# Strassen's scheme moved from the down projections to the gate and up projections of both SwiGLU layers

## The chip, the cores and the metric

The kernel runs on one core of a Trainium2 chip. Times are microseconds (us) of that core for one launch; the hardware profiler also records one execution, whose span (first to last instruction) and own time are given below. TensorE is PE in the rows, its weight loads PEld, VectorE DVE, ScalarE ACT, GpSimd POOL, and SP is the engine whose queue issues the loads.

## The reference

One decoder layer on 512 tokens of width 1024, all in float32: a SwiGLU layer, a token mixer (a gated linear recurrence beside stick-breaking attention, not touched here), and a second SwiGLU layer. The inner width of a SwiGLU layer is 2816.

```python
def _swiglu(x, w_gate, w_up, w_down):
    return (jax.nn.silu(x @ w_gate) * (x @ w_up)) @ w_down

x = x + 0.5 * _swiglu(_rms_norm(x, ffn1_norm), ffn1_w_gate, ffn1_w_up, ffn1_w_down)
...   # the mixer
x = x + 0.5 * _swiglu(_rms_norm(x, ffn2_norm), ffn2_w_gate, ffn2_w_up, ffn2_w_down)
```

## The kernel before

Activations lie transposed: 8 tiles (k = 0 to 7) of 128 channels x 512 tokens. The inner width is cut into 22 blocks of 128, taken in chunks of 6, 6, 6 and 4 blocks (`CHUNKS`). SwiGLU layer "a" is the first, "b" the second; the letter is in the names of the tiles (`pga`, `l_gb`), and so is the number of the block or chunk in the source's names, which the profile leaves out.

Every float32 operand is split in two: a rounded high part (a cast on ACT) and the remainder (a subtraction on DVE), and every product is made of three matmuls, high x high, high x low, low x high (`mm3`, and the three-fold loop in `product`). `weights` loads a weight tile through the SP queue and `parts` splits it; the split tiles have four buffers each (`wh`, `wl`), so the split of a weight tile waits until PE has used the tile four places before it.

`products(f)` makes gate and up of one block plainly: 2 matrices x 8 k x 3 matmuls of 512 columns. `hidden` multiplies by the norm factor `rb`, applies silu as a sigmoid and a product, and multiplies gate by up. The norm factor comes late (`rsqrt`, `spread`), so the first blocks are multiplied before it is there.

The down projection of the first three chunks uses Strassen's scheme in Winograd's form (7 products instead of 8): the 2 x 2 blocks are the inner blocks f and f+1 of a pair, the output tiles k and k+4, and the two halves of 256 tokens. `operands` makes the activations' seven combinations of a pair and splits them (`bh`, `bl`); `down` adds the weights (`sums`, DVE), splits four groups of them, and runs 7 products of m = 3 pairs x 3 matmuls of 256 columns, each collected into `x` by DVE (`collect`, L350). The last chunk of 4 blocks goes down plainly (`down_plain`).

The order on each engine is made when the program is built: a scheduler takes the instructions in the order of the source and issues those that are ready first by its own model; on the chip each engine then runs its list in that order. `products` of the next chunk stands ahead of a chunk's down projection, so that PE has work while the activations are combined.

Of the kernel before, what the change touches and what calls it, by code (L numbers as in the profile page):

```python
# [28 lines left out]

ORDER = (0, 4, 1, 5, 2, 6, 3, 7)  # L30
# [19 lines left out]
def hybrid_layer_kernel(  # L50
# [160 lines left out]

    def ffn(name, xn, wg, wu, wd, first, done):
        def products(f, between=None):
            n = f"{name}{f}"
            gh, gl = weights(wg[f], f"g{n}")
            uh, ul = weights(wu[f], f"u{n}")
# [16 lines left out]
        with tc.tile_pool(name=f"ffn_{name}", bufs=2, reuse_waits="tile") as fp:  # L233

            def hidden(f, out_):

                n = f"{name}{f}"
                if f == len(ahead):
                    ahead.append(products(f))
                pg, pu = ahead[f]  # L240
                g = fp.tile([P, T], F32, tag="g", name=f"gg{n}")
                nc.vector.tensor_mul(g, pg, rb)
                sg = fp.tile([P, T], F32, tag="sg", name=f"sg{n}")
                nc.scalar.activation(sg, g, AF.Sigmoid)
                u = fp.tile([P, T], F32, tag="u", name=f"uu{n}")
                nc.vector.tensor_mul(u, pu, rb)  # L246
                nc.vector.tensor_mul(u, u, g)
                hidden.last = nc.vector.tensor_mul(out_, halves(u), halves(sg))

            def halves(ap):  # L250
                return ap.rearrange("p (c t) -> p c t", c=2)

            def operands(f, i):

                n = f"{name}{f}"

                b = fp.tile([P, 8, TH], F32, tag="b", name=f"b{n}")
                hidden(f, b[:, 0:2, :][:, ::-1, :])
                hidden(f + 1, b[:, 2:4, :])
                nc.vector.tensor_sub(  # L260
                    b[:, 4:8:2, :], b[:, 1:4:2, :], b[:, 0:1, :].to_broadcast([P, 2, TH])
                )
                for o, t, m in ((5, 4, 3), (7, 5, 2)):
                    nc.vector.scalar_tensor_tensor(
                        b[:, o, :], b[:, t, :], -1.0, b[:, m, :], op0=ALU.mult, op1=ALU.subtract
                    )
                h = fp.tile([P, 7, TH], F32R, tag=f"bh{i}", name=f"bh{n}", bufs=1)
                l = fp.tile([P, 7, TH], F32R, tag=f"bl{i}", name=f"bl{n}", bufs=1)
                for c in (slice(0, 3), slice(3, 7)):
                    r = b[:, c.start + 1 : c.stop + 1, :]  # L270
                    nc.scalar.copy(h[:, c, :], r)
                    nc.vector.tensor_sub(l[:, c, :], r, f32(h[:, c, :]))
                return h, l

            def plain(f, i):

                n = f"{name}{f}"
                b = fp.tile([P, 2, TH], F32, tag="h", name=f"hf{n}")
                hidden(f, b)
                if i % 2 == 0:  # L280
                    plain.tiles = [
                        fp.tile([P, 7, TH], F32R, tag=f"b{c}{i // 2}", name=f"h{c}{n}", bufs=1) for c in "hl"
                    ]
                h, l = (t[:, i % 2 * 2 : i % 2 * 2 + 2, :] for t in plain.tiles)
                nc.scalar.copy(h, b)
                nc.vector.tensor_sub(l, b, f32(h))
                return h.rearrange("p c t -> p (c t)"), l.rearrange("p c t -> p (c t)")

            def down_plain(k, col, nf, hs):

                n = f"{name}{col}_{k}"
# [17 lines left out]
                if done is not None:  # L309
                    done(k)  # L310
# [645 lines left out]
```

## Time and profile before

| | |
|---|---|
| time, median of 3 runs | 944.76 us (939.89 to 945.4) |
| profiled execution | 943.62 us, span 941.8 us |
| granted TensorE clock | 0.995 |
| busy: PE, PEld, DVE, ACT, POOL | 927.3, 785.5, 670.6, 374.1, 110.9 us |
| loaded from memory | 86.54 MB |
| layer a, mixer, layer b (by the chain's rows) | about 0 to 350, 350 to 585, 585 to 942 us |

Matmuls are pipelined: the duration of one (390 ns for 512 columns, 284 ns for 256) is longer than the distance from its start to the next one's start, so work on PE is counted here by distances of starts. The same holds in a small way for DVE, whose instructions start some 0.08 us before the one ahead has ended.

### The profile page before, as it was taken

What the parts mean: (1) busy time and instruction counts of PE and PEld (TensorE: products, weight loads), DVE (VectorE), ACT (ScalarE), POOL (GpSimd) and SP (SyncE); (2) the same over time, 40 slices, a digit from 0 to 9 for tenths busy, and PEclk for the clock granted to TensorE, in tenths of its full rate; (3) what the DMA queues carried; (4) which work ended last, traced back from release to release, by engine and by line L of the source; (5) the groups of instructions that cost most, each with busy time, mean ns of one, the idle gap of its engine ahead of it and who ended that gap; (6) DMA issues with size and microseconds to landing.
All of it is one profiled execution on the core that took longest, in us unless ns stands there. A gap on an engine that the chain in (4) does not pass through costs nothing.

```text
span 941.8 us, 12498 instructions
## 1 busy us (share of the span) xinstructions
PE 927.3 (98%) x4906; PEld 785.5 (83%) x4906; DVE 670.6 (71%) x1001; ACT 374.1 (40%) x528; POOL 110.9 (12%) x79
## 2 busy tenths in 40 slices
PE   8999999999999999999999999999999999999998
PEld 6888988898889888888776567888988899889987
DVE  7696867686768649855768868387766777677753
ACT  7233433333333326446556744343333334333430
POOL 4000000000000004644431140500000000000000
PEclk9999999999999999999998999999999999999999
DMA  7530342035202423322110122421253125212312
GB/s 246 179 112 1 130 162 94 19 114 178 90 23 68 142 82 112 112 89 90 34 56 24 46 80 93 164 90 45 68 179 104 53 68 179 90 68 68 111 46 90
DMA packets 27066, 89.44 MB, mean 95 GB/s; under 512 B 3072, under 2 KB 5376, under 8 KB 27008
## 3 DMA queue, kind: packets, MB, share of 16 engines
q1 hardware_dynamic: 27008, 88.65, 27.6%
q8 instruction: 39, 0.64, 0.3%
q14 instruction: 19, 0.16, 0.0%
HBM read 86.54 MB, written 2.10 MB: 94 GB/s over the span
## 4 chain that ended last, share of the span: by engine, by line
PE 90%; DVE 4%; issue 2%; DMA 1%; ACT 1%; POOL 1%; SPq 1%; DVEq 0%; ACTq 0%; POOLq 0%
PE pda L343 10%; PE pdb L343 9%; PE pga L137 5%; PE pga L138 5%; PE pga L139 5%; PE pub L137 4%; PE pub L138 4%; PE pub L139 4%; PE pgb L137 4%; PE pgb L139 4%; PE pgb L138 4%; PE pua L138 4%; PE pua L137 4%; PE pua L139 4%; PE po L137 1%
## 5 line engine op out<-in xcount | busy, mean ns | idle before, releaser
L343 PE MATMUL pdb<-bhb,h_db 128*128 128x256 f32 x252 | 71.2, 284 | 0.0
L343 PE MATMUL pda<-bha,h_da 128*128 128x256 f32 x252 | 71.2, 284 | 0.0
L343 PE MATMUL pdb<-blb,h_db 128*128 128x256 f32 x252 | 71.0, 283 | 0.0
L343 PE MATMUL pda<-bla,h_da 128*128 128x256 f32 x252 | 71.0, 283 | 0.0
L343 PE MATMUL pdb<-bhb,l_db 128*128 128x256 f32 x252 | 70.5, 284 | 0.2 <-DVE l_db L129 0.2
L343 PE MATMUL pda<-bha,l_da 128*128 128x256 f32 x252 | 70.4, 283 | 0.0
L137 PE MATMUL pub<-xh_b,h_ub 128*128 128x512 f32 x176 | 68.7, 390 | 0.5 <-DVE yo L704 0.5
L137 PE MATMUL pgb<-xh_b,h_gb 128*128 128x512 f32 x176 | 68.7, 390 | 0.0
L139 PE MATMUL pgb<-xh_b,l_gb 128*128 128x512 f32 x176 | 68.5, 389 | 0.0
L139 PE MATMUL pub<-xh_b,l_ub 128*128 128x512 f32 x176 | 68.5, 389 | 0.0
L138 PE MATMUL pgb<-xl_b,h_gb 128*128 128x512 f32 x176 | 68.5, 389 | 0.0
L138 PE MATMUL pub<-xl_b,h_ub 128*128 128x512 f32 x176 | 68.5, 389 | 0.0
L137 PE MATMUL pga<-xh_a,h_ga 128*128 128x512 f32 x160 | 62.4, 390 | 0.0
L137 PE MATMUL pua<-xh_a,h_ua 128*128 128x512 f32 x160 | 62.3, 390 | 0.0
L139 PE MATMUL pga<-xh_a,l_ga 128*128 128x512 f32 x160 | 62.3, 389 | 0.0
L138 PE MATMUL pga<-xl_a,h_ga 128*128 128x512 f32 x160 | 62.3, 389 | 0.0
L139 PE MATMUL pua<-xh_a,l_ua 128*128 128x512 f32 x160 | 62.3, 389 | 0.0
L138 PE MATMUL pua<-xl_a,h_ua 128*128 128x512 f32 x160 | 62.2, 389 | 0.0
L167 POOL TENSOR_TENSOR sqa_m<-sqa_m,sq_m 128x512 f32<-128x512 f32 x7 | 11.8, 1679 | 325.4 <-issue 321.5
L246 DVE TENSOR_TENSOR uub<-pub,rb_b 128x512 f32<-128x512 f32 x22 | 15.2, 690 | 47.3 <-PE pub L139 47.3
L343 PEld LDWEIGHTS pda<-bha,h_da 128*128 128x128 f32 x252 | 48.3, 192 | 0.5
L343 PEld LDWEIGHTS pdb<-bhb,h_db 128*128 128x128 f32 x252 | 48.2, 191 | 0.5
(317 smaller groups left out, 2454.5 us busy)
## 6 DMA issues: line engine op xcount, KB each, us to landing
r_gb<-in_wg SPq DMA_DIRECT2D x22, 512.0 KB, 3.2
r_ub<-in_wu SPq DMA_DIRECT2D x22, 512.0 KB, 3.2
r_ga<-in_wg SPq DMA_DIRECT2D x20, 512.0 KB, 3.3
r_ua<-in_wu SPq DMA_DIRECT2D x20, 512.0 KB, 3.4
rda<-in_wd SPq DMA_DIRECT2D x12, 768.0 KB, 4.3
rdb<-in_wd SPq DMA_DIRECT2D x12, 768.0 KB, 4.5
x<-in_xT SPq DMA_DIRECT2D x8, 256.0 KB, 4.9
r_da<-in_wd SPq DMA_DIRECT2D x4, 512.0 KB, 3.5
```

Source lines behind the costliest of these rows:

```text
L137: nc.tensor.matmul(out_, wh, ah, start=start, stop=False)
L138: nc.tensor.matmul(out_, wh, al, start=False, stop=False)
L139: nc.tensor.matmul(out_, wl, ah, start=False, stop=stop)
L167: nc.gpsimd.tensor_add(self.acc, self.acc, sq)
L246: nc.vector.tensor_mul(u, pu, rb)
L343: nc.tensor.matmul(pt, p[:, s], a, start=start and i == 0 and q == 0, stop=i == m - 1 and q == 2, skip_group_check=True,)
```

## The change

The first three pairs of inner blocks (`PLAIN = 6` blocks) go through gate and up plainly, as before. The eight pairs from the seventh block on go by Strassen's scheme: the 2 x 2 blocks are now two neighbouring tiles k of the input's channels, the two inner blocks of the pair, and the two halves of the tokens. The input's combinations are made once in each layer (`operands`, 4 pairs of k, now with the norm factor multiplied in ahead), held in 14 pairs of tiles, and used by all eight pairs. The weights' sums are made for each pair and matrix (`matrix`: one load of 1 MB, four additions of 128x512, then the split in four groups). A product is 4 x 3 matmuls of 256 columns; the two accumulators of a matrix (`px`, `py`, one bank each) are read out after every product, by a copy on ACT (`keep`) or an addition on DVE (`add`). Gate and up alternate (`g0 g1 u0 u1 ...`). Silu is now one function on ACT. The down projection is plain everywhere: 8 k x (blocks of the chunk) x 3 matmuls of 512 columns. The layout of the weights in memory follows, and `ORDER` is gone.

```diff
-ORDER = (0, 4, 1, 5, 2, 6, 3, 7)
+PLAIN = 6
...
-        with tc.tile_pool(name=f"ffn_{name}", bufs=2, reuse_waits="tile") as fp:
...
+        with tc.tile_pool(name=f"ffn_{name}", bufs=1, reuse_waits="tile") as fp:
...
+            def split(u, p, i):
+                n = f"{name}{p}"
+                h = fp.tile([P, 2, T], F32R, tag=f"hh{i}", name=f"hh{n}")
+                l = fp.tile([P, 2, T], F32R, tag=f"hl{i}", name=f"hl{n}")
+                for t in range(2):
+                    src = flat(u[:, 2 * t : 2 * t + 2, :])
+                    nc.scalar.copy(h[:, t, :], src)
+                    nc.vector.tensor_sub(l[:, t, :], src, f32(h[:, t, :]))
+                return [(h[:, t, :], l[:, t, :]) for t in range(2)]
+            def plain(p, i):
+                g, u = pair_tiles(p)
+                for t in range(2):
+                    f = 2 * p + t
+                    if f == len(ahead):
+                        ahead.append(products(f))
+                    gg, uu = flat(g[:, 2 * t : 2 * t + 2, :]), flat(u[:, 2 * t : 2 * t + 2, :])
+                    pg, pu = ahead[f]
+                    nc.vector.tensor_mul(gg, pg, rb)
+                    nc.scalar.activation(gg, gg, AF.Silu)
+                    nc.vector.tensor_mul(uu, pu, rb)
+                    nc.vector.tensor_mul(uu, uu, gg)
+                return split(u, p, i)
+            held = {}
+            def operands():
+                extra = [6]
+                def tiles(n):
+                    if extra[0]:
+                        extra[0] -= 1
+                        i = extra[0]
+                        return [fp.tile([P, 2, TH], F32R, tag=f"x{c}{i}", name=f"x{c}_{n}") for c in "hl"]
+                    return [
+                        xpool.tile([P, 2, TH], F32R, tag=f"x{c}", name=f"x{c}_{n}", bufs=8) for c in "hl"
+                    ]
+                for k in range(KD // 2):
+                    n = f"s{name}{k}"
+                    b = fp.tile([P, 8, TH], F32, tag="b", name=f"b{n}")
+                    for kk, o in ((2 * k, b[:, 0:2, :][:, ::-1, :]), (2 * k + 1, b[:, 2:4, :])):
+                        h, l = (f32(p[kk]).rearrange("p (c t) -> p c t", c=2) for p in (xn.h, xn.l))
+                        nc.vector.tensor_add(o, h, l)
+                        nc.vector.tensor_mul(o, o, rb.rearrange("p (c t) -> p c t", c=2))
+                    nc.vector.tensor_sub(
+                        b[:, 4:8:2, :], b[:, 1:4:2, :], b[:, 0:1, :].to_broadcast([P, 2, TH])
+                    )
+                    for o, t, m in ((5, 4, 3), (7, 5, 2)):
+                        nc.vector.scalar_tensor_tensor(
+                            b[:, o, :], b[:, t, :], -1.0, b[:, m, :], op0=ALU.mult, op1=ALU.subtract
+                        )
+                    for s in (B11, B22, T2, T4):
+                        if s == T4 and k % 2:
+                            h, l, o = *operands.last, 1
+                        else:
+                            h, l = tiles(f"{n}_{s}")
+                            o = 0
+                        w = 1 if s == T4 else 2
+                        if w == 1:
+                            operands.last = h, l
+                        src = b[:, s + 1 : s + 1 + w, :]
+                        nc.scalar.copy(h[:, o : o + w, :], src)
+                        nc.vector.tensor_sub(l[:, o : o + w, :], src, f32(h[:, o : o + w, :]))
+                        for i in range(w):
+                            held[k, s + i] = h[:, o + i, :], l[:, o + i, :]
+            def matrix(w, c, p):
+                n = f"{c}{name}{p}"
+                q = 4 * P
+                raw = fp.tile([P, 4, q], F32, tag="raw", name=f"r{n}", bufs=3)
+                nc.sync.dma_start(raw, w[p].rearrange("p (s w) -> p s w", s=4))
+                sums = fp.tile([P, 3, q], F32, tag="sums", name=f"s{n}", bufs=2)
+                nc.vector.tensor_add(sums[:, 1, :], raw[:, 2, :], raw[:, 0, :])
+                s1 = raw[:, 0, :]
+                nc.vector.tensor_add(s1, s1, raw[:, 1, :])
+                nc.vector.tensor_add(sums[:, 0, :], raw[:, 2, :], s1)
+                nc.vector.tensor_add(sums[:, 2, :], raw[:, 3, :], sums[:, 0, :])
+                groups = [
+                    [raw[:, 2:4, :]],
+                    [sums[:, 0:1, :], raw[:, 0:1, :]],
+                    [sums[:, 1:3, :]],
+                    [raw[:, 1:2, :]],
+                ]
+                ws = []
+                def get(group):
+                    if group < len(ws):
+                        return ws[group]
+                    width = sum(a.shape[1] for a in groups[group]) * q
+                    hi = wpool.tile([P, width], F32R, tag="wh", name=f"h_{n}{group}", bufs=4)
+                    lo = wpool.tile([P, width], F32R, tag="wl", name=f"l_{n}{group}", bufs=4)
+                    o = 0
+                    for a in groups[group]:
+                        a = flat(a)
+                        to = slice(o, o + a.shape[1])
+                        nc.scalar.copy(hi[:, to], a)
+                        nc.vector.tensor_sub(lo[:, to], a, f32(hi[:, to]))
+                        o += a.shape[1]
+                    ws.append((hi, lo))
+                    return hi, lo
+                px, py = (bank(f"p{i}{n}", "b")[:, :TH] for i in "xy")
+                def product(pt, group, half, b, start):
+                    wh, wl = get(group)
+                    for k in range(KD // 2):
+                        s = slice((half * 4 + k) * P, (half * 4 + k + 1) * P)
+                        bh, bl = held[k, b]
+                        for i, (l, r) in enumerate(((wh, bh), (wh, bl), (wl, bh))):
+                            nc.tensor.matmul(
+                                pt, l[:, s], r, start=start and k == 0 and i == 0,
+                                stop=k == KD // 2 - 1 and i == 2, skip_group_check=True,
+                            )
+                return [
+                    (px, 0, 0, B11, True), (py, 0, 1, B21, True),
+                    (px, 1, 0, T2, False), (py, 1, 1, T1, True),
+                    (px, 2, 0, T3, False), (py, 2, 1, B22, False),
+                    (px, 3, 0, T4, False),
+                ], product
+            def fast(p, i):
+                g, u = pair_tiles(p)
+                def keep(o, c):
+                    def after(pt):
+                        nc.scalar.copy(o[:, c, :], pt)
+                    return after
+                def add(o, c):
+                    def after(pt):
+                        nc.vector.tensor_add(o[:, c, :], pt, o[:, c, :])
+                    return after
+                def last_gate(pt):
+                    nc.scalar.activation(g[:, 2, :], pt, AF.Silu, scale=-1.0)
+                both = {}
+                for c, w, o, end in (("g", wg, g, last_gate), ("u", wu, u, keep(u, 2))):
+                    after = [keep(o, 0), add(o, 0), keep(o, 1), keep(o, 3), add(o, 3), add(o, 1), end]
+                    steps, product = matrix(w, c, p)
+                    both[c] = [(product, *z) for z in zip(steps, after)]
+                for c in "g0 g1 u0 u1 g2 g3 u2 u3 g4 g5 u4 g6 u5 u6".split():
+                    product, step, after = both[c[0]][int(c[1])]
+                    product(*step)
+                    after(step[0])
+                    if c == "g5":
+                        nc.scalar.activation(flat(g[:, 0:2, :]), flat(g[:, 0:2, :]), AF.Silu)
+                        nc.scalar.activation(g[:, 3, :], g[:, 3, :], AF.Silu, scale=-1.0)
+                nc.vector.tensor_mul(u[:, 0:2, :], u[:, 0:2, :], g[:, 0:2, :])
+                nc.vector.scalar_tensor_tensor(
+                    u[:, 2:4, :], u[:, 2:4, :], -1.0, g[:, 2:4, :], op0=ALU.mult, op1=ALU.mult
+                return split(u, p, i)
             f0 = 0
+            for nf in CHUNKS:
+                hs = []
                 for i in range(nf // 2):
+                    p = f0 // 2 + i
+                    hs += (plain if 2 * p < PLAIN else fast)(p, i)
+                last = f0 + nf == NF
+                for k in range(KD):
+                    n = f"{name}{f0}_{k}"
+                    per = 2 if last else 1
+                    if k % per == 0:
+                        src = wd[k : k + per, :, f0 * P : (f0 + nf) * P].rearrange("k p m -> p k m")
+                        two = weights(src, f"d{n}", per * nf * P, per)
+                    wh, wl = (w[:, k % per * nf * P : (k % per + 1) * nf * P] for w in two)
+                    cuts = (0, TH, T) if last and done is None and k == KD - 1 else (0, T)
+                    for t0, t1 in zip(cuts, cuts[1:]):
+                        t = slice(t0, t1)
+                        pt = bank(f"pd{n}_{t0}", "y")
+                        for i in range(nf):
+                            s = slice(i * P, (i + 1) * P)
+                            mm3(pt[:, t], wh[:, s], wl[:, s], hs[i][0][:, t], hs[i][1][:, t], i == 0, i == nf - 1)
+                        nc.vector.scalar_tensor_tensor(
+                            x[k][:, t], pt[:, t], 0.5, x[k][:, t], op0=ALU.mult, op1=ALU.add
+                        )
+                        if last and done is None:
+                            nc.sync.dma_start(out[:, k, t], x[k][:, t])
+                    if last and done is not None:
+                        done(k)
+                if f0 == 0:
+                    operands()
                 f0 += nf
```

Three places in the engines' orders. The first is the start of layer a on DVE, right after the blocks that are multiplied before the norm factor is there. `first_p` are the four accumulators of the first two blocks, `pga` that of the third, `rb_a` the norm factor, `l_ga` split weights of gate. Before:

```order
L129 TENSOR_TENSOR l_ga_459<-r_ga_455,h_ga_457 128x1024
L129 TENSOR_TENSOR l_ua_465<-r_ua_461,h_ua_463 128x1024
L182 TENSOR_SCALAR m_a<-pst_a 128x4
L129 TENSOR_TENSOR l_ga_539<-r_ga_535,h_ga_537 128x1024
L242 TENSOR_TENSOR gga_421<-first_p_118,rb_a 128x512
L246 TENSOR_TENSOR uua_425<-first_p_122,rb_a 128x512
L242 TENSOR_TENSOR gga_429<-first_p_126,rb_a 128x512
```

and now, where `bsa` is the input's combinations, `rga` and `rua` the 1 MB loads of the first Strassen pair's gate and up weights, `sga` and `sua` their sums:

```order
L128 TENSOR_TENSOR l_ga_446<-r_ga_442,h_ga_444 128x1024
L128 TENSOR_TENSOR l_ua_452<-r_ua_448,h_ua_450 128x1024
L295 TENSOR_TENSOR bsa_862<-xh_a_155,xl_a_157 128x2x256
L295 TENSOR_TENSOR bsa_862<-xh_a_167,xl_a_169 128x512
L181 TENSOR_SCALAR m_a<-pst_a 128x4
L326 TENSOR_TENSOR sga_958<-rga_956 128x512
L328 TENSOR_TENSOR rga_956<-rga_956 128x512
L329 TENSOR_TENSOR sga_958<-rga_956 128x512
L330 TENSOR_TENSOR sga_958<-rga_956,sga_958 128x512
L128 TENSOR_TENSOR l_ga_520<-r_ga_516,h_ga_518 128x1024
L326 TENSOR_TENSOR sua_967<-rua_965 128x512
L267 TENSOR_TENSOR gga_420<-first_p_118,rb_a 128x512
```

Two additions of the input's combinations and five of the weights' sums now stand ahead of the first reading of `first_p` (L242 before, L267 now).

The second is the same place in SP's queue of loads. Before (`rda` are 768 KB of down weights) and now:

```order
L122 DMA r_ua_541<-in_wu 128x1024
L122 DMA r_ga_605<-in_wg 128x1024
L320 DMA rda_0_746<-in_wd 128x1536
L320 DMA rda_1_754<-in_wd 128x1536
L122 DMA r_ua_611<-in_wu 128x1024
L122 DMA r_ga_684<-in_wg 128x1024
```

```order
L121 DMA r_ua_522<-in_wu 128x1024
L121 DMA r_ga_582<-in_wg 128x1024
L324 DMA rga_956<-in_wg 128x2048
L324 DMA rua_965<-in_wu 128x2048
L324 DMA rga_1204<-in_wg 128x2048
L121 DMA r_ua_588<-in_wu 128x1024
L121 DMA r_da_0_654<-in_wd 128x768
```

Three loads of 1 MB of gate and up weights stand where two of 768 KB of down weights stood, ahead of the sixth block's up weights (`r_ua`).

The third is DVE in the middle of the work by Strassen's scheme in layer a. Before, in the first chunk's down projection (`sda` sums, `l_da` split weights, L350 the collecting into `x`):

```order
L129 TENSOR_TENSOR l_da_0_3_908<-rda_0_746,h_da_0_3_906 128x384
L350 SCALAR_TENSOR_TENSOR x_92<-pda_1_0_760,x_92 128x256
L350 SCALAR_TENSOR_TENSOR x_96<-pda_1_1_761,x_96 128x256
L129 TENSOR_TENSOR l_da_1_3_922<-rda_1_754,h_da_1_3_920 128x384
L350 SCALAR_TENSOR_TENSOR x_95<-pda_0_0_752,x_95 128x256
L350 SCALAR_TENSOR_TENSOR x_91<-pda_0_1_753,x_91 128x256
L323 TENSOR_TENSOR sda_2_936<-rda_2_934 128x768
L350 SCALAR_TENSOR_TENSOR x_96<-pda_1_0_760,x_96 128x256
L129 TENSOR_TENSOR l_da_2_0_952<-rda_2_934,h_da_2_0_950 128x768
L326 TENSOR_TENSOR sda_2_936<-rda_2_934,sda_2_936 128x384
L350 SCALAR_TENSOR_TENSOR x_92<-pda_1_1_761,x_92 128x256
```

and now, from the first pair's end into the second's beginning (`l_ga`, `l_ua` split weights of gate and up, L386 the additions from the accumulators, L406 gate by up):

```order
L350 TENSOR_TENSOR l_ga_1223<-rga_1204,h_ga_1222 128x1024
L386 TENSOR_TENSOR uua_955<-pxua_972,uua_955 128x256
L328 TENSOR_TENSOR rua_1213<-rua_1213 128x512
L329 TENSOR_TENSOR sua_1215<-rua_1213 128x512
L350 TENSOR_TENSOR l_ua_1253<-rua_1213,h_ua_1252 128x1024
L386 TENSOR_TENSOR uua_955<-pyua_973,uua_955 128x256
L330 TENSOR_TENSOR sua_1215<-rua_1213,sua_1215 128x512
L350 TENSOR_TENSOR l_ga_1283<-sga_1206,h_ga_1282 128x512
L350 TENSOR_TENSOR l_ga_1283<-rga_1204,h_ga_1282 128x512
L406 TENSOR_TENSOR uua_955<-uua_955,gga_954 128x512
```

Splits, sums and readings of accumulators still alternate. A step of before has 7 sums and splits of weights for 7 readings, a pair now has 18 for 6. The names with `rga` and `rua` on both sides of the arrow are sums made in place.

More of the change, by code (lines that the diff above doesn't have):

```diff
@@ L199, in spread @@
             self.rb = rb
+    B11, B21, B22, T1, T2, T3, T4 = range(7)
     def ffn(name, xn, wg, wu, wd, first, done):
@@ new lines, in ffn, with flat, pair_tiles @@
+        with tc.tile_pool(name=f"ffn_{name}", bufs=1, reuse_waits="tile") as fp:
+            def flat(ap):
+                return ap.rearrange("p c t -> p (c t)")
+            def pair_tiles(p):
+                n = f"{name}{p}"
+                g = fp.tile([P, 4, TH], F32, tag="g", name=f"gg{n}", bufs=2)
+                u = fp.tile([P, 4, TH], F32, tag="u", name=f"uu{n}")
+                return g, u
+            def split(u, p, i):
+                n = f"{name}{p}"
+                h = fp.tile([P, 2, T], F32R, tag=f"hh{i}", name=f"hh{n}")
[134 more added lines that the diff above has]
+                    u[:, 2:4, :], u[:, 2:4, :], -1.0, g[:, 2:4, :], op0=ALU.mult, op1=ALU.mult
+                )
+                return split(u, p, i)
@@ L370, in ffn @@
             f0 = 0
-            for nf in CHUNKS[:-1]:
-                bs, after = [], None
+            for nf in CHUNKS:
+                hs = []
                 for i in range(nf // 2):
-                    bs.append(operands(f0 + 2 * i, i))
-                    after = hidden.last if i == nf // 2 - 2 else after
-                f0 += nf
-                ahead.append(products(f0))
-                for k in range(0, KD // 2, 2):
-                    two = [list(down(k + i, (f0 - nf) // 2, nf // 2, bs, after)) for i in range(2)]
-                    for r in (slice(0, 2), slice(2, 4), slice(4, 6), slice(6, 7)):
-                        for steps in two:
-                            for step in steps[r]:
-                                step()
@@ L385, in ffn @@
-            hs = [plain(f0 + i, i) for i in range(NF - f0)]
-            for k in ORDER:
-                down_plain(k, f0 // 2, NF - f0, hs)
+                    p = f0 // 2 + i
[22 more added lines that the diff above has]
+                        done(k)
@@ L411, in first_products @@
                 for i, (w, f) in enumerate(ws):
-                    nc.sync.dma_start(raw[i][:, s], w[f][:, s])
+                    nc.sync.dma_start(raw[i][:, s], w[0][:, f * KD * P :][:, s])
                 nc.sync.dma_start(x[2 * kk + 1], xT[:, 2 * kk + 1, :])
@@ L508, in project @@
         if j == 0:
-            order = [(i, k) for k in ORDER for i in range(2)]
+            order = [(i, k) for k in range(KD) for i in range(2)]
         for i, k in order:
@@ L885, in by_pairs @@
     def by_pairs(w):
-        b = by_block(w).reshape(KD, P, NF, P)
-        o, f0 = [], 0
-        for nf in CHUNKS:
-            order = [f0 + i for i in (*range(0, nf, 2), *range(1, nf, 2))]
-            if f0 + nf == NF:
-                order = range(f0, NF)
-            half = [b[c : c + KD // 2][:, :, order].reshape(KD // 2, P, nf * P) for c in (0, KD // 2)]
-            o += half
-            f0 += nf
-        return np.concatenate(o, axis=2)
+        o = by_block(w).reshape(NF, P, KD, P)
+        o = np.concatenate([o[:, :, 0::2], o[:, :, 1::2]], axis=2).reshape(NF, P, KD * P)
+        o = np.concatenate([o[1::2], o[0::2]], axis=2)
+        b = by_block(w)
+        o[: PLAIN // 2] = np.concatenate([b[0:PLAIN:2], b[1:PLAIN:2]], axis=2)
+        return o
     w = np.asarray(w_in)[0]
```

134 lines of the change are left out of this document (9 added, 125 removed).

## The prediction

> **What bounds the kernel now.** I read the page's busy shares and slices first, then what PE waits for, then stretches by stage.
>
> ```profile
> PE 927.3 (98%) x4906; PEld 785.5 (83%) x4906; DVE 670.6 (71%) x1001; ACT 374.1 (40%) x528; POOL 110.9 (12%) x79
> PE   8999999999999999999999999999999999999998
> DVE  7696867686768649855768868387766777677753
> PEclk9999999999999999999998999999999999999999
> PE 90%; DVE 4%; issue 2%; DMA 1%; ACT 1%; POOL 1%; SPq 1%; DVEq 0%; ACTq 0%; POOLq 0%
> ```
>
> PE is busy at 9 tenths in all but the first, second and last slices, at the full granted clock, and the chain that ended last runs over it for 90%. What it waits for is little, by the waits of PE (engine, line, waited for; us, times, longest):
>
> ```profile
> PE pw L773 <- DVE be L765: 3.3, 3, 1.5
> PE pv L137 <- DVE natk L639: 2.4, 1, 2.4
> ...
> PE pdb L343 <- DVE l_db L129: 0.2, 1, 0.2
> ```
>
> The first two lie in the mixer; of the SwiGLU layers behind their start only 0.2 us is left. So here the time is the number of matmuls by the distance between them, as long as what feeds PE stays hidden. Both scales come from the stretches (length; busy us and count of PE, PEld, DVE, ACT, POOL) and from starts on PE:
>
> ```profile
> 87.00:117.00 30.00, 30.00 (x248) 29.78 (x247) 26.20 (x50) 11.80 (x16) 0.00 (x0) 1.00 0.28 95
> 117.00:183.00 66.00, 66.00 (x298) 54.83 (x297) 43.88 (x58) 21.48 (x26) 0.00 (x0) 1.00 0.29 101
> 98.20:113.40 15.20, 15.20 (x128) 15.11 (x127) 14.58 (x28) 5.82 (x9) 0.00 (x0) 1.00 0.20 65
> ```
>
> ```profile
> 329.60 0.39 PE L138 MATMUL pua<-xl_a,h_ua 128*128 128x512 f32 x1
> ...
> 344.79 0.39 PE L139 MATMUL pda<-hha,l_da 128*128 128x512 f32 x1
> ```
>
> ```profile
> 87.36 29.29 PE pda L343 x243
> ```
>
> Of 512 columns there are 68 matmuls from the one row to the other: 15.19 / 67 = **226.7 ns** each. Of 256 columns, 29.29 / 243 = **120.5 ns**, 7 ns over the half; the weight loads fill 29.78 of 30 us there and 54.83 of 66 in the plain stretch, so a matmul of 256 columns is held by its weight load. Keep the third stretch in mind: for 15 us DVE was busy at 96% and PE didn't stop.
>
> **The change part by part. PE first.** In each layer gate and up lose 16 blocks x 2 matrices x 8 k x 3 = 768 matmuls of 512 columns, and get 8 pairs x 2 matrices x 7 products x 4 x 3 = 1344 of 256. The down projections lose Strassen's 3 x 252 = 756 of 256 and get 18 blocks x 8 x 3 = 432 of 512. In both layers together: 672 of 512 columns fewer, 1176 of 256 columns more.
>
> 672 x 226.7 ns = 152.3 us go; 1176 x 120.5 ns = 141.7 us come. **PE's work falls by 10.6 us.** By the matmuls' arithmetic it would be 42 x 2 units of 512 columns, 19 us; the weight loads of the 256-column form take nearly half of that back.
>
> [...] The rows above measure 226.7 and 120.5 ns on this kernel's float32 operands, so the sum goes by them.
>
> **DVE in a pair.** A pair takes PE 168 x 120.5 ns = 20.2 us. DVE does in it 8 sums of 128x512, splits of 4 x 1024 and 6 x 512 columns, 6 additions of 128x256 from the accumulators, and 4 operations of 512 (gate by up, and the split of the result). What each occupies is the distance of starts in a full queue:
>
> ```profile
> 40.57 0.68 DVE L246 TENSOR_TENSOR uua<-first_p,rb_a 128x512 f32<-128x512 f32 x1
> 41.16 0.68 DVE L242 TENSOR_TENSOR gga<-first_p,rb_a 128x512 f32<-128x512 f32 x1
> ...
> 45.96 1.22 DVE L129 TENSOR_TENSOR l_ua<-r_ua,h_ua 128x1024 fp32r<-128x1024 f32 x1
> 47.09 0.69 DVE L260 TENSOR_TENSOR ba<-ba 128x512 f32<-128x512 f32 x1
> ...
> 49.17 0.42 DVE L264 SCALAR_TENSOR_TENSOR ba<-ba 128x256 f32<-128x256 f32 x1
> 49.50 0.69 DVE L248 TENSOR_TENSOR ba<-uua,sga 128x512 f32<-128x512 f32 x1
> ```
>
> 0.60, 1.13 and 0.33 us: 18 x 0.60 + 4 x 1.13 + 6 x 0.33 = **17.3 us of 20.2**, 86%. That is below the 96% at which PE ran on, but for 60 us in a chunk instead of 15; DVE may stand idle for 2.9 us of a pair, no more. In the chunk's down projection, 144 x 226.7 ns = 32.6 us, it has only 8 splits and 8 readings and catches up, as far as the four weight buffers let it. ACT is no limit:
>
> ```profile
> L127 ACT CAST h_ga<-r_ga 128x1024 fp32r<-128x1024 f32 x24 | 25.2, 1049 | 35.7 <-PE pga L138 26.2 <-PE pda L343 4.9 <-PE pq L139 2.4
> L244 ACT ACTIVATE sga<-gga 128x512 f32<-128x512 f32 x22 | 13.9, 630 | 8.0 <-DVE gga L242 7.8
> L783 ACT COPY wt<-pw 128x256 f32<-128x256 f32 x8 | 3.1, 390 | 1.9 <-PE pw L773 1.9
> L575 ACT ACT_TABLE_LOAD x1 | 1.3, 1283 | 0.0
> ```
>
> Casts 4 x 1.05 + 6 x 0.63, 7 copies from accumulators at 0.39, silu 0.39 x 2 + 0.63, the result's casts 2 x 0.63: 13.4 us of 20.2. The order has three more table loads (silu against sigmoid), 1.28 us each, on an engine with a third of its time free: nothing on PE.
>
> **The ring of buffers.** A split starts only when PE has left the tile four places back. The narrowest place by the order is where a pair ends: u's third group is left after product u5, and the next pair's u0, in the same buffer, begins 36 matmuls later, 4.3 us. Cast 1.05 and split 1.22 need 2.3. At the other groups I find 1 to 2 us in the same way. The loads of 1 MB fit too, by the page's loads (KB, median us to landing):
>
> ```profile
> r_gb<-in_wg SPq DMA_DIRECT2D x22, 512.0 KB, 3.2
> rda<-in_wd SPq DMA_DIRECT2D x12, 768.0 KB, 4.3
> ```
>
> 1 MB lands then in some 5.4 us (an estimate from these two), into the third raw buffer, about half a pair ahead; the bytes are the same as before. I put waits inside the pairs at 1.5 us in all (0.1 a pair), since the margins are thin; bounds 0, and 27 (the slower rival).
>
> **The input's combinations,** for each of 4 pairs of k 8 operations of 512 and 3 of 256 columns, 4 x 5.8 = 23 us of DVE in a layer, stand in the order between the plain blocks' work and the first chunk's down projection. From the first reading of `first_p` to the first product of Strassen's kind, DVE has 91 instructions, 56 us by these distances, PE 288 matmuls of 512 columns, 65 us; layer b has more room. Hidden. Should the cover be gone, those on the path would be the last pair of k's operations, some 6 us a layer.
>
> **The first blocks of layer a.** Here a term is exposed. PE's fourth block needs the accumulator that DVE's first L242 frees:
>
> ```profile
> 33.31 0.33 SPq L122 DMA_DIRECT2D r_ga<-in_wg  x1
> 33.69 0.94 SPq L320 DMA_DIRECT2D rda<-in_wd  x2
> ...
> DMA to landing us min/median/max: 5.4/6.1/6.7
> ...
> 39.97 0.68 DVE L242 TENSOR_TENSOR gga<-first_p,rb_a 128x512 f32<-128x512 f32 x1
> ...
> 43.68 0.39 PE L137 MATMUL pga<-xh_a,h_ga 128*128 128x512 f32 x1
> ```
>
> Today it reads at 40.0 and PE comes at 43.7. Now the sums stand ahead of it. The two `rda` landed 5.4 us after 33.7 and 6.7 after 34.2, at 39.1 and 40.9: 256 KB in 0.6 us. So the first 1 MB lands at 39.7, the second at 42.1. Four sums end at 42.1, a split at 43.2, the next sum at 43.8, the reading at 44.5: PE waits **0.9 us** (from 0, if the loads are quicker by 1, to 3).
>
> **The ends.** After a pair's last product PE has 29 matmuls of the down projection that need only the earlier blocks (by the order), 6.6 us; copy, product, cast and split of the last block take 0.39 + 0.69 + 2 x 0.63 + 0.69, 3 us. At the last pair of a layer 28 stand there. The mixer's order is unchanged, and so is the kernel's end. Nothing else is lost or won.
>
> **Sum:** 941.8 - 10.6 + 0.9 + 1.5 = 933.6 us of span; with the 1.8 us around it, **935.4**. The median of the runs shown is 1.1 us above the profiled execution, so I say **936**, 0.9% below 944.8. A measurement of this kernel tells about 1% from no change: this sits just inside.
>
> **The rivals.** *Nothing waits.* The floor of PE's work, with no wait in the pairs and none at the start: 943.6 - 10.6 = 933 us; for it speak the full PE at 96% of DVE, against it that the margins are 1 to 2 us in 16 pairs of 14 products. *The gain is eaten.* Each pair loses 0.3 to 0.9 us, where an ACT copy from an accumulator stands ahead of a cast that PE needs: 16 x 0.6 = 10 us, 943 to 945. It shows as PE idle before L363, released by ACT or DVE.
>
> *DVE sets the pace (slower).* If DVE, in order and waiting in turn for ACT's casts and PE's products, stands idle for more than 14% of a pair, it takes over: 17.3 / 0.86 = 20.2 us is the point. In the stretch 87 to 117 it was idle for 13% while PE was full, though for the most part because nothing was due. At 21% a pair takes 21.9 us, 16 x 1.7 = 27 us more than PE's work: 960, slower by 1.7%. Against it: a queue that had work was filled to 96%.
>
> *The matmuls of 256 columns run slower here.* The gain is gone at 2688 d - 1512 x 120.5 = 672 x 226.7, d = 124.4 ns, and 132 ns makes it 2% slower. Against it, the rows of both layers differ by less than 1 ns:
>
> ```profile
> 278.77 29.27 PE pda L343 x243
> ...
> 757.80 29.25 PE pdb L343 x243
> ```
>
> [...]
>
> **How the numbers follow.** Forecast (932 to 940): 0.57. Nothing waits (930 to 935): 0.13. Gain eaten (940 to 950): 0.15. DVE sets the pace (950 to 970): 0.10. Slower matmuls: 0.05 (940 to 965). The range 931 to 950 leaves out the last two's upper parts and a little below. Faster by over 1% is below 935.3: nothing waits, and under half of the forecast's own spread, 0.38; slower by over 1% is above 954.2: 0.11; within, 0.51.
>
> **What would show it.** PE in the profile after: 748 x 3 rows of `mm3` and 2688 of L363, starts 120.5 ns apart; idle before L363 under 3 us in sum; one wait near 44 us for the fourth block's accumulator, released by DVE; DVE near 86% in the pairs' stretches. I am wrong if PE's idle time in the pairs is tens of us (then see whether ACT or DVE ended it), if the distance there is not 120.5, or if the chain leaves PE for the input's combinations.

## The result: 0.6% less, with two waits in it that the change brought

| | before | after |
|---|---|---|
| median of 20 runs | 942.79 us | 936.65 us |
| ratio, 95% interval | | 0.9936 [0.9923, 0.9949] |
| profiled execution: time, span | 943.62, 941.8 us | 937.35, 935.6 us |

The forecast was 936. One of the 20 runs of the kernel before took 1163.69 us and is left out of the ratio. The page of the changed kernel, busy shares and chain:

```profile
PE 916.2 (98%) x5410; PEld 800.3 (86%) x5410; DVE 677.0 (72%) x1007; ACT 443.3 (47%) x739; POOL 109.6 (12%) x79
PE 87%; DVE 6%; DMA 2%; issue 2%; ACT 1%; POOL 1%; SPq 0%; DVEq 0%; ACTq 0%; POOLq 0%
```

PE's busy time fell by 11.1 us, and the chain runs over it for 87% instead of 90%. Where it leaves PE is seen in the waits of PE (us, times, longest):

```profile
PE pw L828 <- DVE be L820: 3.3, 3, 1.5
PE pga L136 <- DVE gga L267: 2.9, 1, 2.9
PE pga L136 <- DVE x L433: 2.9, 1, 2.9
PE pv L136 <- DVE natk L694: 2.5, 1, 2.5
```

The first and the last stood there before. The two `pga` are new: the first is the fourth block's gate accumulator in layer a, the second the mixer's first gate accumulator. No row of L363, the products of Strassen's scheme, is among the waits. The stretches of pairs, in the same columns as before:

```profile
130.20:150.50 20.30, 20.30 (x171) 20.30 (x170) 17.50 (x28) 11.93 (x22) 0.00 (x0) 1.00 0.20 65
150.50:171.00 20.50, 20.50 (x171) 20.44 (x170) 18.16 (x30) 12.27 (x23) 0.00 (x0) 1.00 0.34 119
```

PE is full in both, DVE at 86 and 89%. What the work on PE is worth can be read from layer b, which has no new wait; its first and last matmul, after the change and before it:

```profile
583.69 0.39 PE L136 MATMUL pgb<-xh_b,h_gb 128*128 128x512 f32 x1
...
932.29 0.28 PE L138 MATMUL pdb<-hhb,l_db 128*128 128x256 f32 x1
```

```profile
583.38 0.39 PE L137 MATMUL pgb<-xh_b,h_gb 128*128 128x512 f32 x1
...
938.55 0.28 PE L139 MATMUL pdb<-hhb,l_db 128*128 128x256 f32 x1
```

348.60 against 355.17 us: 6.57 us less in one layer, with the granted clock at 1.00 throughout in both, so some 13 us for two. The spans differ by 6.2. About 7 us of the gain are given back, at the two `pga`.

**The first wait, at the start of layer a.** DVE, then PE (start, duration, operation; in brackets the idle time before it and what ended it):

```profile
40.70 0.69 DVE L326 TENSOR_TENSOR sga<-rga 128x512 f32<-128x512 f32 x1 [6.69 <-DMA rga<-in_wg]
41.43 0.69 DVE L328 TENSOR_TENSOR rga<-rga 128x512 f32<-128x512 f32 x1
...
44.62 0.68 DVE L326 TENSOR_TENSOR sua<-rua 128x512 f32<-128x512 f32 x1
45.23 0.68 DVE L267 TENSOR_TENSOR gga<-first_p,rb_a 128x512 f32<-128x512 f32 x1
```

```profile
45.97 0.50 PE L136 MATMUL pga<-xh_a,h_ga 128*128 128x512 f32 x1 [2.91 <-DVE gga L267]
...
46.92 0.63 PE L136 MATMUL pga<-xh_a,h_ga 128*128 128x512 f32 x1
47.35 0.63 PE L137 MATMUL pga<-xl_a,h_ga 128*128 128x512 f32 x1
```

DVE stands idle for 6.7 us until the 1 MB load is there, makes five sums and a split, and only then reads the accumulator that PE's fourth block needs. And behind the wait the matmuls are 0.43 us apart instead of 0.227. The stretches there show why, in the third column from the right, the granted clock:

```profile
46.00:48.00 2.00, 2.00 (x6) 1.63 (x7) 2.00 (x4) 1.44 (x3) 0.00 (x0) 0.64 0.55 219
48.00:50.00 2.00, 2.00 (x6) 1.54 (x6) 2.00 (x4) 1.71 (x3) 0.00 (x0) 0.51 0.00 0
50.00:52.00 2.00, 2.00 (x11) 1.64 (x10) 2.00 (x4) 1.38 (x3) 0.00 (x0) 1.00 0.00 0
```

For some 3.4 us the clock is at half. The 24 matmuls of the block's gate take 7.2 us, where 24 x 0.2267 are 5.4: 1.7 us more.

**The second wait, from layer a to the mixer:**

```profile
361.12 0.39 PE L138 MATMUL pda<-hha,l_da 128*128 128x512 f32 x1
361.34 0.39 PE L136 MATMUL pxr<-xh_m,h_xr 128*128 128x512 f32 x1
...
365.09 0.47 PE L136 MATMUL pga<-xh_m,h_ga 128*128 128x512 f32 x1 [2.90 <-DVE x L433]
```

```profile
362.59 0.68 DVE L433 SCALAR_TENSOR_TENSOR x<-pda,x 128x512 f32<-128x512 f32 x1
363.19 1.15 DVE L152 SCALAR_TENSOR_TENSOR xl_m<-x,vec,xh_m 128x512 fp32r<-128x512 f32 x1
364.26 0.68 DVE L433 SCALAR_TENSOR_TENSOR x<-pda,x 128x512 f32<-128x512 f32 x1
```

The mixer's first `pga` waits for DVE's reading of the last down accumulator, 3 us behind PE. In the kernel before, DVE's last reading came as late, and `pga` did not wait for it:

```profile
363.38 0.39 PE L137 MATMUL pxr<-xh_m,h_xr 128*128 128x512 f32 x1
...
364.06 0.39 PE L137 MATMUL pga<-xh_m,h_ga 128*128 128x512 f32 x1
```

```profile
366.33 0.68 DVE L304 SCALAR_TENSOR_TENSOR x<-pda,x 128x512 f32<-128x512 f32 x1
```

The kernel's accumulators take turns in the banks of PSUM, those of the down projections in four of them, and the program has PE wait with a new one until the last one in that bank has been read: in the rows above DVE's reading ends at 364.94, and `pga` begins 0.15 us later. By the allocations of the two built programs, `pga` takes PSUM bank 5 in both. Before, bank 5 held the first and the fifth of the last chunk's eight down accumulators; the new rotation (4, 6, 7, 5, 4, 6, 7, 5) puts the eighth there. Neither the diff nor the engines' orders show this.

### The profile page after: what moved, and what is told of

It is laid out like the page before. It is cut to its first block, busy times and chain, and to the rows that moved or that the text cites. A ratio compares the mean times of both kernels' runs of the same rounds, so it can differ in the third digit from the quotient of the medians.

```text
span 935.6 us, 13626 instructions
## 1 busy us (share of the span) xinstructions
PE 916.2 (98%) x5410; PEld 800.3 (86%) x5410; DVE 677.0 (72%) x1007; ACT 443.3 (47%) x739; POOL 109.6 (12%) x79
## 4 chain that ended last, share of the span: by engine, by line
PE 87%; DVE 6%; DMA 2%; issue 2%; ACT 1%; POOL 1%; SPq 0%; DVEq 0%; ACTq 0%; POOLq 0%
PE pxgb L363 5%; PE pxga L363 5%; PE pxub L363 5%; PE pxua L363 5%; PE pdb L136 4%; PE pdb L137 4%; PE pdb L138 4%; PE pda L136 4%; PE pda L138 4%; PE pda L137 4%; PE pyga L363 4%; PE pygb L363 4%; PE pyua L363 4%; PE pyub L363 4%; PE pga L136 1%
## 5 line engine op out<-in xcount | busy, mean ns | idle before, releaser
L137 PE MATMUL pdb<-hlb,h_db 128*128 128x512 f32 (+1 forms) x180 | 68.9, 385 | 0.0
L138 PE MATMUL pdb<-hhb,l_db 128*128 128x512 f32 (+1 forms) x180 | 68.7, 385 | 0.0
L137 PE MATMUL pda<-hla,h_da 128*128 128x512 f32 x176 | 68.2, 389 | 0.0
L138 PE MATMUL pda<-hha,l_da 128*128 128x512 f32 x176 | 68.0, 389 | 0.0
L136 PE MATMUL pdb<-hhb,h_db 128*128 128x512 f32 (+1 forms) x180 | 67.3, 385 | 0.0
L136 PE MATMUL pda<-hha,h_da 128*128 128x512 f32 x176 | 66.7, 389 | 0.0
L363 PE MATMUL pxga<-xl_sa,h_ga 128*128 128x256 f32 x128 | 36.2, 283 | 0.0
L363 PE MATMUL pxga<-xh_sa,l_ga 128*128 128x256 f32 x128 | 36.2, 283 | 0.0
L363 PE MATMUL pxgb<-xh_sb,l_gb 128*128 128x256 f32 x128 | 36.2, 283 | 0.0
L363 PE MATMUL pxgb<-xl_sb,h_gb 128*128 128x256 f32 x128 | 36.2, 283 | 0.0
L363 PE MATMUL pxub<-xh_sb,l_ub 128*128 128x256 f32 x128 | 36.2, 283 | 0.0
```

The costliest lines, as they stand in the source:

```text
L136: nc.tensor.matmul(out_, wh, ah, start=start, stop=False)
L137: nc.tensor.matmul(out_, wh, al, start=False, stop=False)
L138: nc.tensor.matmul(out_, wl, ah, start=False, stop=stop)
L363: nc.tensor.matmul(pt, l[:, s], r, start=start and k == 0 and i == 0, stop=k == KD // 2 - 1 and i == 2, skip_group_check=True,)
```

## The experiments

Every ratio is to the kernel before, on the same chip in the same series.

**The changed kernel again,** unedited, beside the next three.

> The changed kernel once more, as the measure for the three runs beside it. It should be 0.993 to 0.995 of the kernel before (936 to 938 us), with two waits of PE of 2.9 us, at 46 us (before the fourth block's first matmul) and at 365 us (before the mixer's first gate matmul). Open is the granted clock behind the first wait, 0.51 to 0.64 for some 3 us in the profiled execution: if the wait causes the drop, a profile that has the wait mostly shows a drop behind it; if the drop is chance, it comes at any place or not at all.

Measured: 936.37 us, ratio 0.9932 [0.9915, 0.9949]. The waits were 3.1 and 2.9 us, and this time the clock fell at both (0.50 for some 3.4 us from 44.5, within the wait that ended at 45.1, and again from 365.4). The mean granted clock of this execution, 0.991, is some 17 us at 0.50, five such falls, where the first profile had three. The other three lie in the mixer, which the change does not touch: it took 225.1 us (222.35 in the first profile), while the stretch ahead of the first wait took 42.0 us (43.1), layer a from the fourth block 315.1 (315.4) and layer b 348.6 (348.6).

**The start alone** (e_start):

```diff
-                    nc.vector.tensor_mul(uu, pu, rb)
+                    plain.read = nc.vector.tensor_mul(uu, pu, rb)
+                    if f == 1:
+                        plain.freed = plain.read
...
+                with tc.issue_after(plain.freed.ins):   # around matrix's four sums
```

> The four sums of every Strassen pair's weights may be issued only after DVE has read the first two blocks' accumulators. Theory: at the start of layer a the sums, which wait for the 1 MB loads, hold DVE's reading back; with the reading ahead of them it comes at 40 to 41 us, PE's wait of 2.9 us at 46 goes, and with it the low clock behind it (1.7 us): 2.9 to 4.6 us less than the changed kernel, 932 to 934 us. Rival A: the sums now come late for the first pair of Strassen's scheme, and PE waits there instead: no gain, 936 to 937, with idle time of PE before L365 in the first chunk's pair. Rival B: the norm factor, not the sums, is late: the wait stays above 2 us with another releaser.

Measured: 932.63 us, 0.9892 [0.9875, 0.9909]; 3.7 us less than the changed kernel beside it, inside the 2.9 to 4.6. In the profiled execution DVE reads at 39.14, PE goes on, and the clock stays:

```profile
39.14 0.68 DVE L267 TENSOR_TENSOR gga<-first_p,rb_a 128x512 f32<-128x512 f32 x1
```

```profile
42.85 0.39 PE L136 MATMUL pga<-xh_a,h_ga 128*128 128x512 f32 x1
...
356.50 0.39 PE L136 MATMUL pxr<-xh_m,h_xr 128*128 128x512 f32 x1
```

```profile
44.00:46.00 2.00, 2.00 (x10) 1.68 (x9) 2.00 (x5) 1.19 (x3) 0.00 (x0) 1.00 0.42 172
46.00:48.00 2.00, 2.00 (x10) 1.66 (x9) 2.00 (x3) 1.08 (x2) 0.00 (x0) 1.00 0.00 0
```

From the fourth block to the mixer layer a takes 313.65 us (before, from 43.68 to its first `pxr` at 363.38: 319.70). That is 6.05 less, near layer b's 6.57. No wait appeared in the first pair (rival A), nor was the norm factor late (rival B).

**The bank alone** (e_bank):

```diff
+                if last and done is not None:
+                    for s in range(3):
+                        nc.tensor.matmul(bank(f"skip{name}{s}", "y")[:, 0:1], ones, ones[:, 0:1], ...)
                 for k in range(KD):
```

> Three matmuls of one column, in accumulators of their own from the same four banks, are put ahead of layer a's last down projection. They move its eight accumulators on by three banks, so that the mixer's first gate accumulator gets a bank which was read four tiles earlier. Theory: the wait of 2.9 us at 365 us is a wait for a bank, and goes; 2.9 us less than the changed kernel, 933 to 934 us. Rival: DVE is late there in any case (its additions into x and the splits for the mixer run 3 us behind PE), and PE waits within the next 8 us for a split of the input's last tiles: no gain, 936 to 937.

Measured: 935.14 us, 0.9914 [0.9899, 0.993]. The wait at the mixer is gone; the stretch 360 to 368 of this kernel, and of the changed one:

```profile
360.00:368.00 8.00, 8.00 (x37) 6.60 (x36) 8.00 (x12) 4.76 (x9) 5.35 (x4) 1.00 0.12 33
```

```profile
360.00:368.00 8.00, 5.10 (x23) 3.95 (x22) 8.00 (x12) 5.93 (x11) 4.30 (x4) 1.00 0.10 33
```

But the time fell by 1.2 us, not 2.9, and the two intervals overlap, so alone this is not shown by the times. The three added matmuls cost some 0.7 us themselves (with them layer a takes 314.32 us from the fourth block to the mixer in the next run, without them 313.65 in the one above). In the profiled execution the wait at the start was longer, too (3.5 us; the 1 MB load landed at 41.2 instead of 40.7). The rest is within what the clock does from one execution to the next, as the next run shows.

**Both** (e_both):

> Both edits. If the two waits are independent, the gains add up: 5.8 to 7.5 us less than the changed kernel, 929 to 931 us, 0.985 to 0.988 of the kernel before, with PE busy for over 98.5% of the span and no wait of PE above 1 us outside the mixer. If what the first saves is waited for later (the rival), it is like the better one of the two alone, 933.

Measured: 929.86 us, **0.9858 [0.9839, 0.9877]**, 6.5 us below the changed kernel and the fastest here. The bank takes 2.8 us off what the start alone had left, so its 2.9 are there once the start is quiet. The expectation missed in two small things: PE is busy for 98.47% of the span, and the head, which the edits leave alone, has waits above 1 us. The largest waits of PE that are left are two in the mixer, as before, and one in the head:

```profile
PE pw L834 <- DVE be L826: 3.3, 3, 1.5
PE pv L136 <- DVE natk L700: 2.4, 1, 2.4
PE first_p L491 <- DVE xl_a L152: 1.6, 1, 1.6
```

Without its two side effects the change is worth 13.9 us in this series, where the changed kernel had 7.4.

The executions differ in how often the clock falls: their mean granted clock in this series lies between 0.991 and 0.998. The span times the mean granted clock, averaged over a kernel's executions, estimates the span without the falls (roughly, since a fall can cover idle time): 937.4 us before, 929.7 for the changed kernel, 927.3 with the start alone, 927.2 with the bank alone, 924.2 with both. By this estimate the start gives 2.4 us, the bank 2.5 alone and 3.1 on top of the start, and both together leave 13.2 us between the kernel and the one before, close to twice layer b's 6.57.

**Does PE's idle time bring the low clock?** (e_warm, from the changed kernel.) After `ahead.append(products(len(ahead), xn.spread))`:

```diff
+        if first:
+            busy = bank("busy", "y")
+            for _ in range(12):
+                nc.tensor.matmul(busy, xn.h[0][:, :P], xn.h[1], start=True, stop=True)
```

> From the changed kernel: twelve matmuls of 512 columns of the input's first tiles, into an accumulator of their own that nobody reads, stand on PE ahead of the fourth block, where PE waits 2.9 us. They take 12 x 0.2267 = 2.7 us, so the wait stays for DVE's reading, but PE is busy in nearly all of it. Theory (PE's idle time brings the low clock): the granted clock is 1.00 from 44 to 53 us, the fourth block starts where it did (45 to 46.5 us), and the time falls by the 1.7 us of the slow matmuls, in part of the executions: 0.991 to 0.993 of before, 935 to 936 us. Rival (the drop has another cause, such as the loads or DVE's load at that time): 0.50 to 0.64 for 3 us as before, and no change, 0.9935.

Measured: 938.15 us, 0.9927 [0.9909, 0.9945], which tells nothing of a difference. The one profile speaks for the theory: the fourth block still starts at 45.6, and the clock there stays at 1.00, while in the same execution it falls behind the untouched wait at the mixer:

```profile
46.00:48.00 2.00, 2.00 (x11) 1.62 (x10) 2.00 (x5) 1.44 (x3) 0.00 (x0) 1.00 0.35 137
48.00:50.00 2.00, 2.00 (x11) 1.65 (x10) 2.00 (x4) 1.39 (x3) 0.00 (x0) 1.00 0.03 8
...
364.00:366.00 2.00, 2.00 (x6) 1.54 (x6) 2.00 (x5) 1.98 (x5) 0.14 (x1) 0.54 0.00 0
366.00:368.00 2.00, 2.00 (x7) 1.54 (x6) 2.00 (x2) 1.23 (x2) 1.56 (x1) 0.61 0.51 137
```

The sums and loads of that place ran here as well, so in this execution it is PE's idleness that goes with the drop; in the three profiles with the wait unfilled there, the clock fell each time. One profile against three is evidence and no more; the mean granted clock of the six executions, 0.994 as in the changed kernel's, does not decide it.

**What the pairs are worth** (f_plain22, from e_both): `PLAIN = 22`, and `operands()` only where `PLAIN < NF`.

> From the kernel with both edits (e_both, 0.986 of before): all 22 blocks of gate and up go plainly, no input combinations, no sums; the down projections stay plain. Theory (the time is the sum over PE's rows): 16 pairs change from 168 matmuls of 256 columns at 120.0 to 120.5 ns to 96 of 512 at 226.7 ns, 20.2 against 21.76 us, so 16 x 1.5 to 1.6 = 24 to 26 us more: 954 to 956 us, 1.011 to 1.013 of before. Rival (the pairs by Strassen's scheme lose time that the stretches don't show, or DVE's and ACT's load there slows PE): less than 15 us more, under 945.

Measured: 957.24 us, 1.0143 [1.0128, 1.0158], a little more than the theory's upper end. Layer b from its first to its last matmul:

```profile
589.89 0.39 PE L136 MATMUL pgb<-xh_b,h_gb 128*128 128x512 f32 x1
...
951.22 0.28 PE L138 MATMUL pdb<-hhb,l_db 128*128 128x256 f32 x1
```

361.33 us, 12.7 above the 348.6 with eight pairs (of the changed kernel and of e_both alike): 1.59 us a pair, so a pair takes 96 x 0.2267 - 1.59 = 20.17 us, 168 matmuls of 120.1 ns. The scheme gives on PE what its rows say.

**More work on DVE** (f_dve1, f_dve2, f_dve3, from e_both): the last sum of each matrix is made once, twice, three times more.

```diff
+                    for _ in range(2):          # 3 and 4 in the other two
                         nc.vector.tensor_add(sums[:, 2, :], raw[:, 3, :], sums[:, 0, :])
```

> From e_both: the last of a matrix's four weight sums is made twice, so DVE has two more additions of 128x512 in each pair, 1.2 to 1.4 us; its load in a pair rises from 17.3 of 20.15 us (86%) to 18.7 (93%). Theory (PE runs on until DVE's sum exceeds PE's): no change, 929 to 931 us. Rival (the prediction's slower one: DVE in order needs 14% of a pair for its own waits): 18.7 / 0.86 = 21.7 us a pair, 16 x 1.6 = 25 us more, 955.

> The last sum is made three times: 2.4 to 2.9 us more DVE work in a pair, 19.7 to 20.2 of 20.15 us (98 to 100%). Theory: at the edge; 930 to 936 us, with small waits of PE before L366 released by DVE. Rival (14% needed): 23.2 us a pair, 979.

> The last sum is made four times: 3.6 to 4.3 us more, 20.9 to 21.6 us of DVE work in a pair, more than PE's 20.15. Theory: DVE sets the pace in the pairs; 0.8 to 1.5 us each, 12 to 24 us in 16 pairs, less what is made ahead in the first pair of each chunk: 938 to 952 us. Rival (14% needed): 24.7 us a pair, 1000. Rival two (the down projections between the chunks let DVE make up for it, since sums of a later pair can be made ahead): no change, 930.

Measured: 934.09 (0.99 [0.9885, 0.9914]), 931.24 (0.987 [0.9855, 0.9885]) and 938.53 us (0.9946 [0.9929, 0.9962]), beside e_both's 929.86 in another series. The stretch 147 to 167, at the end of a chunk's pairs, of e_both and then of the three:

```profile
147.00:167.00 20.00, 20.00 (x167) 19.91 (x167) 17.52 (x29) 11.73 (x22) 0.00 (x0) 1.00 0.31 112
```

```profile
147.00:167.00 20.00, 19.54 (x160) 19.24 (x160) 18.16 (x30) 11.65 (x22) 0.00 (x0) 1.00 0.26 98
```

```profile
147.00:167.00 20.00, 20.00 (x168) 19.91 (x167) 19.01 (x32) 11.47 (x22) 0.00 (x0) 1.00 0.16 58
```

```profile
147.00:167.00 20.00, 19.17 (x153) 18.36 (x152) 18.76 (x32) 10.90 (x21) 0.00 (x0) 1.00 0.11 38
```

With two more sums a matrix DVE is at 95% and PE doesn't stop: layers a and b take as long as in e_both within 0.1 us. With three, PE waits, but layer b, for one, takes 352.5 us from first to last matmul, 4 more than with no extra sums, at the theory's lower end. The rival's "14% idle" is refuted: its prices were 955, 979 and 1000. The first dose was a surprise: the least work, yet 2.9 us slower than the second. It has a wait that is not DVE's load:

```profile
PE pyga L367 <- ACT gga L385: 0.9, 2, 0.5
```

```profile
156.78 1.05 ACT L353 CAST h_ua<-sua 128x1024 fp32r<-128x1024 f32 x1 [1.95 <-PE pyua L367]
...
158.77 0.36 ACT L385 COPY gga<-pyga 128x256 f32<-128x256 f32 x1
```

A copy from an accumulator stands in ACT's order behind a cast that waits 1.95 us for its weight buffer, and PE's next product waits for the copy, in the third pair of a chunk. These two waits in a layer cost 1.2 us by the distance of starts, and the places right behind them another 0.4; the layers are 1.7 us longer each. The mixer of that execution is 2.7 us longer than e_both's (220.6 against 217.9); the mean granted clock of the execution is 0.995, which is some three falls of 3.4 us, against 0.998, one fall, in e_both's. In f_dve2 the copy runs ahead of that cast (at 157.01 and 158.33), and in f_dve3 too: the three programs differ in ACT's order, not only in DVE's load. Why the scheduler chose this order at the first dose stays open.

**Three weight buffers** (f_bufs3, from e_both): `bufs=4` becomes `bufs=3` at the four allocations of `wh` and `wl`.

> From e_both: three buffers instead of four for the split weights. By the order, with three the narrowest place is where a pair ends: the next pair's first gate group takes the buffer that u's third group leaves after product u5, and only u6 (12 matmuls, 1.44 us) lies before its use, while the cast and split take 1.05 + 1.22 = 2.3 us. Theory (four buffers leave 2 us at the narrowest place, three are 0.9 to 1.3 us short once a pair): 16 x 0.9 to 1.3 = 14 to 21 us more, 944 to 951 us, with waits of PE before L366 released by ACT and DVE. Rival (the splits run so far ahead that the ring is no limit): no change, 930. Second rival (the splits wait in order ahead of DVE's readings of the accumulators, so each short place costs two or three times): over 960.

Measured: 936.15 us, 0.9923 [0.99, 0.9946]: 6 us more, between rival and theory. In the profiled execution layer a is 3.0 us longer than in e_both, layer b 2.7. Layer a shows the expected kind of wait three times, at 0.2 us:

```profile
138.97 0.39 PE L366 MATMUL pxga<-xh_sa,l_ga 128*128 128x256 f32 x1 [0.21 <-DVE l_ga L353]
```

By the distance of starts these three places cost 1.3 us with the matmul behind each; another 1.2 are lost in the first chunk's down projection, where PE waits for a cast of its weights (`h_da`). The mixer uses the same buffers; it has a new wait of 2.1 us at a split and is 1.2 us longer. So the ring matters at three, but in most pairs the next weights were ready in time, where the expectation had each pair 0.9 to 1.3 us short.

**A smaller cover for the input's combinations** (f_plain4, from e_both): `PLAIN = 4`, `CHUNKS = [4, 6, 6, 6]`, and two rows of down weights to a load only in a chunk of 4.

> From e_both: only four blocks of a layer go plainly (the chunks are 4, 6, 6 and 6), so nine pairs instead of eight by Strassen's scheme, and the cover for the input's combinations is two blocks smaller. PE's work falls by 2 x 1.6 = 3.2 us. Theory (the combinations are hidden by the cover alone): from DVE's first reading of an accumulator at 39 us to the first product of Strassen's kind DVE needs some 48 us, PE now has the fourth block and 96 matmuls of the down projection, 33 us: PE waits 8 to 14 us in layer a, and 0 to 10 in layer b; 935 to 951 us. Rival (the combinations were never near the path): 926 to 927, the best of all.

Measured: 945.03 us, 1.0022 [1.0008, 1.0035], though PE's work is 3.2 us less. Each layer has one wait, ended by the cast of the input's last pair of k. The clock falls in its last part and stays low behind it, in layer a from 83.9 to 90.7, of which 85.5 to 90.7 are behind the wait:

```profile
PE pxgb L366 <- ACT xh_sb L316: 5.4, 1, 5.4
PE pxga L366 <- ACT xh_sa L316: 5.4, 1, 5.4
```

```profile
86.00:88.00 2.00, 2.00 (x11) 2.00 (x11) 2.00 (x6) 1.61 (x4) 0.00 (x0) 0.50 0.00 0
88.00:90.00 2.00, 2.00 (x12) 2.00 (x11) 1.84 (x4) 2.00 (x4) 0.00 (x0) 0.50 0.00 0
```

The sum in the expectation was too pessimistic: it held the products back until all four pairs of k were there, and in the trace those of the first pairs run before the wait, the first at 73.4. The 5.4 us are near the "some 6 us a layer" that the prediction gave for a cover that is gone. With six blocks all of it is hidden in both layers.

## Why the prediction came true, and where it did not

The total was right partly by luck, because its errors cancel.

- **PE's work, -10.6 us:** right in kind, too small by 2 to 3. Layer b alone gave 6.57 (5.3 predicted). The matmuls of the new scheme run at 120.0 to 120.1 ns instead of 120.5, which is 0.6 us a layer; the rest of the difference is not resolved. The rival of slower matmuls is out.
- **DVE in a pair, 17.3 of 20.2 us:** 17.5 to 18.2 measured, in stretches of 20.3 and 20.5. That the load is no limit is shown up to 95%.
- **Waits in the pairs, 1.5 us:** none. The fear came from margins read off the order; even with a buffer less, the pairs of layer a lost only 1.3 us in f_bufs3, so the margins were read too thin. The rival of the eaten gain is not in this kernel, but f_dve1 shows its very mechanism under another order.
- **The combinations, hidden:** right, and f_plain4 shows that the cover was needed.
- **The first blocks, 0.9 us:** this term was mis-sized: 2.9 us of wait, within the 0 to 3 stated, and 1.7 us of low clock behind it that no term held. The load landed at 40.7, not 39.7, and the first four sums started 0.73 us apart, not 0.60: each after the first reads what the one ahead wrote, or writes where it read, while operations with nothing in common start 0.60 apart behind them (from 45.23 to 47.62). Putting the sums behind the reading gave 3.7 us. The prediction read the clock as full; in the trace of before it was at 0.50 from 472.5 to 475.9, at the end of a wait of PE of 2.4 us in the mixer and behind it, so that a wait can cost more than its length was there to be read.
- **The ends and the mixer, "nothing else is lost or won":** wrong, by 2.9 us: a term put at nothing. The step that failed is "the mixer's order is unchanged": the order was, the bank behind its first gate accumulator was not. That DVE reads the last accumulators 3 us late was so before as well; it cost nothing while PE needed an older bank.

By stretches of the two profiled executions: PE reaches the fourth block 0.8 us earlier; from there to the mixer layer a takes 1.3 us less (6.05, but for the first wait and its low clock); the mixer takes 2.35 more (222.35 against 220.00, with the second wait, and 6.8 us of clock at 0.50 where before had 10.2); layer b takes 6.57 less. That is 6.3, and the spans differ by 6.2.

A slip without weight: the prediction excepts PE's second slice from the busy ones, which stands at 9 tenths too.

## What to carry to other kernels

A change of the work in one place can turn the rotation of shared accumulator banks in the stages behind it: after such a change, look at the joints between stages for a first matmul that waits for the last reading of the stage before (2.9 us here). Work for later that an in-order engine does while its loads are still on the way should stand behind the reading that frees an accumulator (3.7 us here), and a wait of PE of 2 to 3 us can cost more than itself, here 1.7 us more when the clock fell. Where a predicted total comes true, take the ledger apart by stage before believing the terms.

## What the runs showed of the hardware

The mean granted clock of TensorE is below 1.00 in all 13 profiled executions (0.984 to 0.998). In the stretches of before, after, after_again, e_bank, e_warm and f_plain4 that show a fall it went to 0.50, each time for 3.4 us or twice that. At waits of PE of 2.9 to 3.5 us it fell in five of seven (start of layer a: three of three; mixer's first gate: two of four), at both waits of 5.4 us in f_plain4, and not where matmuls of no use filled the wait (e_warm: 1.00 from 42 to 56). It fell at shorter waits as well. At the wait of 2.4 us before `pv` it fell in before, where `pv`'s matmuls took 405 to 418 ns in the mean; in after it stayed at 1.00 there, and they took 390 to 396 (405 to 422 in f_dve1, f_dve3 and f_plain22, 390 to 397 in e_both and f_dve2). In after it fell at the end of a wait of 1.5 us before `pw` (0.50 from 500.5 to 503.9; the wait ended at 500.6) and 1.7 us behind the end of one of 1.4 us (0.50 from 534.7 to 538.1). So these runs give no length of a wait below which the clock is safe. One fall of 3.4 us costs up to about 1.7 us in matmuls of 512 columns: 24 of them took 7.2 us instead of 5.4 at the start of layer a.
